# A hybrid decoder layer: one sum moved from VectorE to ScalarE and GpSimd, attention's queued steps re-spaced, and read-backs placed two weight pairs ahead

## The chip, the cores and the metric

The kernel runs on one core of a Trainium2 chip. A core has TensorE (PE, the matrix engine), VectorE (DVE), ScalarE (ACT), GpSimd (POOL) and SyncE (SP, which here issues nearly all transfers). The engines run side by side and wait for one another through semaphores. The metric is the time of one execution on the device in microseconds; lower is better. The median of three runs before the change is 1590.85 us.

## The reference

One layer of a decoder is computed for 1024 prompt tokens and 32 sample tokens (8 sequences of 4), with a model width of 1024, all in float32. In short form:

```
u = rmsnorm(x, norm_pre)
aq, af, ai, aog, az, bq, bk, bv, bz, ga, gb = split(u @ w_in)
fg = lb + (1 - lb) * sigmoid(af)                      # branch A: gated recurrence, 8 heads of 128
S[t] = fg[t] * S[t-1] + (1 - fg[t]) x ai[t];  o[t] = silu(aq[t]) . S[t]
oa = rmsnorm(o) * hgrn_norm * sigmoid(aog) * silu(az)
p = softmax with sink(q . k / 8 + relative bias)       # branch B: window 128, 16 query heads, 2 kv heads
ob = (p . v) * silu(bz)
m = sigmoid(ga) * (oa @ w_pa) + sigmoid(gb) * (ob @ w_pb)
x = x + rmsnorm(m @ w_o, norm_post)
x = x + (p_l @ w_ple) * sigmoid(x @ w_ple_gate)
```

It returns x, the final recurrent states and the last 128 keys and values, for prompt and sample tokens.

## The kernel before

Everything is held transposed: features on the 128 partitions, tokens along the free dimension. To keep float32 accuracy every product is made of three matmuls on rounded parts (high x high, high x low, low x high), so "a matmul" below is one 128 x 128 weight tile times 512 tokens.

**The work by stages.** After the norm and a first head (to about 157 us) the kernel goes through the heads of branch A, one per about 83.5 us. Each head has three weight pairs (F with Q, V with the output gate, the widening gate with the merge gate A). Then come one pair for keys and values, eight attention pairs (bq with bz, about 37.3 us each), four pairs for merge gate B (`gate_b`), and from about 1138 us on the plain products of `gemm` (line 1440): w_pa, w_pb, w_o, w_ple and w_ple_gate.

**One weight pair** is `pair_gemm` (line 377). Of the eight blocks along the contraction six are multiplied by a scheme with seven products P1, P5, P6, P3, P7, P2, P4 (nine matmuls each), two blocks plainly (four stretches of six matmuls): 87 matmuls. Three PSUM banks, `a`, `c` and `b`, serve two output columns (0 and 1) and two token halves ("tiles"). Sums that two outputs share are copied out by ACT as `c1`, `p5` and `u2` (line 409). Right after P6 the second column's plain products for the first token half go into bank `b`, and line 456 adds them to the kept `p5`: one DVE instruction that reads the bank. Then P3 follows in bank `c`, P7 in `a`, and P2 in a new tile in the bank of `b`, so P2 can begin only when line 456 has read it. Line 416 makes the outputs (three per pair), DVE again; that of column 1 adds `p5` to `a`, and P4 goes on in `a` after it. `ctile` (line 228) gives passing tiles from a ring of three.

**What is queued beside the pairs.** Branch A's recurrence (`hgrn_chain`, line 836), the attention (`attention`, line 1134) and the sample tokens' attention (line 1239) are generators in three queues. `pair_gemm` calls `tick()` after every `quantum` matmuls (6 in branch A, 2 in attention and `gate_b`) and once at its end; at a tick the first generator of each queue does its next step if its delay, in ticks, has run out. `yield n` sets that delay, `yield <function>` waits until the function is true. PE executes in the order in which the program emits (line 127); the other engines' order, and that of the transfers, is set by a planner that takes an instruction when it would be ready by its own clock.

**Branch A's end** (lines 1001 to 1022): per head 8 + 7 matmuls give `bO`; ACT squares it and sums; then `bs` is taken from the same ring of two PSUM tiles (`double`, `single`, line 713) for the sample tokens, its matmuls (lines 1014 and 1016) follow at once, and the norm comes after.

**Attention** per pair: line 1341 (ACT) and line 1342 (DVE) build `stk` from the first output; `scores` (queue 1) then makes the logits of two of four token groups (lines 1157 and 1161; DVE line 1165, ACT line 1172, DVE line 1179), and again after the third output. `outs` (queue 0) takes each group 15 ticks after its logits (`A_WAIT[1]`): `turn` 0 transposes into the one PSUM tile `pt` (line 1189) and DVE copies it out, `A_WAIT[2]` ticks later `turn` 1 uses the same PSUM tile and ACT copies it, `A_WAIT[3]` ticks later `values` multiplies (line 1204), then `gated` writes the result (line 1210) and sends it off, and `A_WAIT[4]` ticks pass before the next group. `A_WAIT[0]` lies between two logits.

**After attention** `sample_attention` is queued, three `gate_b` pairs run, `drain()` ticks until the queues are empty, the memory of `sp` is closed, and the eight `oar` tiles (branch A's results, written to DRAM earlier) are read into its place; then comes the fourth `gate_b`.

Of the kernel before, what the change touches and what calls it, by code (L numbers as in the profile page):

```python
# [16 lines left out]
ALU = mybir.AluOpType  # L17
# [13 lines left out]
VAR = ("B11", "T1", "T2", "B21", "T3", "B22", "T4")  # L31
QUANTUM = 6
A_QUANTUM = 2
A_WAIT = (7, 15, 2, 3, 2)
H_WAIT = (2, 4, 6)
AHEAD = 3
WARM = (7, 21, 9)
# [83 lines left out]
def tile_decoder_step(ctx: ExitStack, tc: tile.TileContext, x_prompt, x_sample, state_hgrn, cache_k, cache_v,  # L121
# [4 lines left out]
    V, S, G, T, DM = nc.vector, nc.scalar, nc.gpsimd, nc.tensor, nc.sync  # L126
# [61 lines left out]
    def enqueue(gen, delay=1, q=0):  # L188
        queues[q].append([gen, delay])
# [38 lines left out]
    def ctile():  # L228
        return gt.tile([P, HT], F32, name=tname("ct"), tag="ct", bufs=3)
# [147 lines left out]
    def pair_gemm(W, X, eps, quantum=QUANTUM):  # L377


        n = [0]  # L380

        def mm(ps, a, b, start, stop):
            T.matmul(ps, a, b, start=start, stop=stop, skip_group_check=True)  # L383
            n[0] += 1
            if n[0] % quantum == 0:
                tick()

        def product(ps, key, var, start):
            prepared()
            wh, wl = W.v[key]  # L390
            xh, xl = X.v[var]
            for k in range(M):
                for m, (a, b) in enumerate(((wh, xh), (wh, xl), (wl, xh))):
                    mm(ps, a[:, k, :], b[:, k, :], start and k == 0 and m == 0, k == M - 1 and m == 2)

        def plain(ps, j, t, start):
            if not R:
                return
            wh, wl = W.v["R"]
            xh, xl = X.v["R"]  # L400
            sl = slice(HT * t, HT * t + HT)
            for k in range(R):
                i, q = k // (4 - M), k % (4 - M)
                for m, (a, b) in enumerate(((wh, xh), (wh, xl), (wl, xh))):
                    mm(ps, a[:, i, q, j, :], b[:, k, sl], start and k == 0 and m == 0, k == R - 1 and m == 2)

        def kept(tag, ps):
            t = gt.tile([P, HT], F32, name=tname(tag), tag=tag, bufs=1)
            S.copy(t, ps)
            return t  # L410

        def out(j, t, ps, other):
            lo = HT * t
            into = getattr(eps[j], "into", None)
            dst = into(slice(lo, lo + HT)) if into else ctile()
            V.tensor_tensor(dst, ps, other, op=ALU.add)  # L416
            if into is None:
                eps[j](lo, slice(lo, lo + HT), dst)

        if W.plain:  # L420
            for j in range(2):
                ps = [bank(banks[0]), bank(banks[1])]
                banks.append(banks.pop(0))
                banks.append(banks.pop(0))
                for i in range(2):
                    prepared()
                    wh, wl = W.v[i, j]
                    for t in range(2):
                        xh, xl = X.v[(("T3", "B11"), ("B22", "B21"))[i][t]]
                        for k in range(M):  # L430
                            for m, (a, b) in enumerate(((wh, xh), (wh, xl), (wl, xh))):
                                mm(ps[t], a[:, k, :], b[:, k, :], i + k + m == 0, not R and i == 1 and k == M - 1 and m == 2)
                    if i + j == 0:
                        gs, part = sample_products(W.raw, X.s)
                if j == 0:
                    sample_outputs(gs, part, eps)
                for t in range(2):
                    plain(ps[t], j, t, False)
                    eps[j](HT * t, slice(HT * t, HT * t + HT), ps[t])
            tick()  # L440
            return
        ta, tc_, tb = banks
        a = bank(ta)
        product(a, "P1", "B11", True)
        gs, part = sample_products(W.raw, X.s)
        c1 = kept("c1", a)
        c = bank(tc_)
        product(c, "P5", "T1", True)
        p5 = kept("p5", c)
        product(a, "P6", "T2", False)  # L450
        sample_outputs(gs, part, eps)
        u2 = kept("u2", a)
        if R:
            b = bank(tb)
            plain(b, 1, 0, True)
            V.tensor_tensor(p5, b, p5, op=ALU.add)  # L456
        product(c, "P3", "B22", False)
        plain(c, 0, 0, False)
        out(0, 0, c, u2)
        product(a, "P7", "T3", False)  # L460
        out(1, 0, a, p5)
        b = bank(tb)
        product(b, "P2", "B21", True)
        plain(b, 0, 1, False)
        out(0, 1, b, c1)
        product(a, "P4", "T4", False)
        plain(a, 1, 1, False)
        eps[1](HT, slice(HT, NP), a)
        banks[:] = [tc_, tb, ta]
        tick()  # L470
# [365 lines left out]
    def hgrn_chain(h, F4, QP, K, vn, Gt):  # L836
# [123 lines left out]
        b = to_natural(K, kn, S.copy)  # L960
# [7 lines left out]
        b = double()  # L968
# [11 lines left out]
        b = single()  # L980
# [6 lines left out]
        for g in range(2):  # L987
# [5 lines left out]
            b = single()  # L993
# [12 lines left out]
        for c in range(NC):  # L1006
            o = bO[:, c * P:(c + 1) * P]
            T.matmul(o, att[:, c, :], vn[:, c, :], start=True, stop=c == 0)
            if c > 0:
                T.matmul(o, QE[:, c * P:(c + 1) * P], St[:, c - 1, :], start=False, stop=True)  # L1010
        for c in range(NC):
            S.activation(junk, bO[:, c * P:(c + 1) * P], AF.Square, accum_out=ssh[:, c:c + 1])
        bs = single()
# [12 lines left out]
        b = double()  # L1026
# [3 lines left out]
        b = single()  # L1030
# [103 lines left out]
    def attention(c, stk, zt):  # L1134
# [78 lines left out]
        def scores(gs_):  # L1213
            for g in gs_:
# [4 lines left out]
                scored[n] = now[0]  # L1219
                yield A_WAIT[0]  # L1220

        def outs():
            for g in range(4):
                n = 4 * c + g
                yield lambda: n in scored and now[0] >= scored[n] + A_WAIT[1]
                p0 = turn(g, 0)
                yield A_WAIT[2]
                p1 = turn(g, 1)
# [5 lines left out]
                done.add(("out", n))  # L1234
                yield A_WAIT[4]

# [91 lines left out]
    for c in range(KT):  # L1328
        stk, zt, parts_ = [None, None], [None, zt1[:, c % 2, :]], []

        def ep_bq(ci, sl, ps):
            if ci == NP:
                S.activation(qS[:, :, :, c], ps.rearrange("p (b t) -> p b t", b=8), AF.Copy, scale=0.125)
                return
            t = ci // HT
            settle(("logits", 4 * c - 3 + 2 * t))
            s = stk[t] = sp.tile([P, 2, HT], F32R, name=f"stk{c}_{t}", tag=("vn", "G")[t])
            for j in range(2):
                r = slice(64 * j, 64 * j + 64)
                o = slice(64 - 64 * j, 128 - 64 * j)  # L1340
                S.activation(s[r, j, :], ps[r], AF.Copy, scale=-0.125)
                V.scalar_tensor_tensor(s[o, j, :], ps[r], -0.125, s[r, j, :], op0=ALU.mult, op1=ALU.subtract)  # L1342
            if t == 0:
                parts_[:] = attention(c, stk, zt)
                enqueue(parts_[0](range(2)), 1, q=1)
                enqueue(parts_[1](), 1)
            else:
                enqueue(parts_[0](range(2, 4)), 1, q=1)

        def ep_bz(ci, sl, ps):  # L1350
            if ci == 0:
                settle(("out", 4 * c - 3))
                zt[0] = sp.tile([P, HT], F32, name=f"zt0_{c}", tag="vS")
            if ci == HT:
                settle(("out", 4 * c - 5))
            d = ctile()[:, :32] if ci == NP else zt[ci // HT]
            S.activation(d, ps, AF.Tanh, scale=0.5)
            V.scalar_tensor_tensor(zS[:, c, :] if ci == NP else d, d, 1.0, ps, op0=ALU.add, op1=ALU.mult)
            done.add(("zt", c, ci // HT))

        pair_gemm(b_pairs[c], u, (ep_bq, ep_bz), quantum=A_QUANTUM)


    def gate_b(p):
        def ep_gb(i):
            def ep_(ci, sl, ps):
                sg = ctile()[:, :ps.shape[-1]]
                S.activation(sg, ps, AF.Tanh, scale=0.5)
                V.tensor_scalar(sg, sg, 0.5, 0.5, op0=ALU.mult, op1=ALU.add)
                DM.dma_start(gb_d[i][:, sl], sg)  # L1370
            return ep_

        pair_gemm(gb_pairs[p], u, (ep_gb(2 * p), ep_gb(2 * p + 1)), quantum=A_QUANTUM)

    enqueue(sample_attention(), 1)
    for p in range(3):
        gate_b(p)
    drain()
    aps_es.close()
# [3 lines left out]
    def load_staged(d, n):  # L1383
        out = []
        for i in range(KT):
            out.append(stg.tile([P, NTOK], F32, name=f"{n}{i}", tag=f"s{i}"))
            DM.dma_start(out[i], d[i])
        return out

    oar = load_staged(oa_d, "oar")  # L1390
    gate_b(3)
    for es in (xv_es, gt_es, wp_es, psg_es):
        es.close()
# [282 lines left out]
```

## Time and profile before

| | us |
|---|---|
| median of three runs (lowest, highest) | 1590.85 (1590.65, 1591.33) |
| the profiled execution's own time | 1589.28 |
| its span, first to last instruction | 1587.5 |

| stage | window, us | length | PE busy | DVE busy | ACT busy | POOL busy |
|---|---|---|---|---|---|---|
| a head of branch A | 324.6 to 408.0 | 83.4 | 81.18 | 57.36 | 36.12 | 33.72 |
| another attention pair | 914.3 to 951.6 | 37.3 | 35.27 | 27.08 | 20.20 | 8.15 |
| start of the plain products | 1138.4 to 1167.3 | 28.9 | 16.10 | 22.80 | 19.60 | 0.00 |
| plain products | 1167.3 to 1440.0 | 272.7 | 272.67 | 87.83 | 59.41 | 0.00 |
| the last stage | 1487.0 to 1587.5 | 100.5 | 96.00 | 34.08 | 25.55 | 0.00 |

Matmuls are pipelined: one of 512 columns lasts about 0.39 us in the records, while the next starts 0.227 us after it. So the start times carry the pace, and a row's bracket, [idle before <- releaser], says how long the engine stood still before it and what ended that. The granted clock of TensorE is 0.988 on average over the execution.

### The profile page before, as it was taken

The page shows a single profiled execution, that of the slowest core. Times are in us where ns is not written, and L with a number is a line of the kernel's source. Part 1 is how long each engine was busy: PE and PEld are TensorE (multiplying, and loading weights), DVE is VectorE, ACT ScalarE, POOL GpSimd, SP SyncE. Part 2 cuts the span into 40 slices and gives each one's busy share as a digit, 9 for nine tenths or more (in the row PEclk, how much of TensorE's full clock was granted, in tenths as well). Part 3 has the DMA queues.
Part 4 walks back from the last instruction along what each step waited for, and adds up shares of the span by engine and source line. Part 5 has one row for each costly group of instructions (what it writes and reads, how often), then busy time and mean ns, then how long its engine had stood idle before and what let it go on. Part 6 is the DMA issues. An engine that isn't in the chain of part 4 may idle for free.

```text
span 1587.5 us, 27717 instructions
## 1 busy us (share of the span) xinstructions
PE 1511.3 (95%) x10569; PEld 1260.0 (79%) x10569; DVE 959.8 (60%) x2102; ACT 653.5 (41%) x1639; POOL 425.9 (27%) x381
## 2 busy tenths in 40 slices
PE   8989999999999999999999999999789999998998
PEld 7767777778787777777666666667689999998998
DVE  7777767585858585764777777754452254227532
ACT  6334444444443534344555555543431122333422
POOL 1374444334353434345222222213100000004100
PEclk9999999999999999999999999999899999999999
DMA  5212121313021212213111111135354544103321
GB/s 181 67 30 87 48 82 42 96 41 96 29 82 55 82 55 69 68 50 93 44 47 47 50 48 47 43 91 194 121 199 138 147 123 146 58 24 100 108 81 55
DMA packets 197249, 129.55 MB, mean 82 GB/s; under 512 B 46324, under 2 KB 184749, under 8 KB 197101
## 3 DMA queue, kind: packets, MB, share of 16 engines
q1 hardware_dynamic: 196300, 127.54, 27.0%
q8 instruction: 83, 1.36, 0.4%
q14 instruction: 50, 0.40, 0.1%
q0 software_dynamic: 672, 0.18, 0.1%
q10 hardware_dynamic: 144, 0.07, 0.0%
HBM read 96.89 MB, written 31.88 MB: 81 GB/s over the span
## 4 chain that ended last, share of the span: by engine, by line
PE 67%; DVE 19%; ACT 5%; issue 4%; POOL 3%; DMA 1%; SPq 1%; DVEq 0%; ACTq 0%; POOLq 0%
PE g L383 29%; PE g L1440 23%; ACT lg L1172 2%; PE po L1204 2%; PE gs L365 2%; DVE QE L893 2%; DVE wl L271 1%; DVE ct L416 1%; PE g L790 1%; POOL vS L991 1%; DVE stk L1342 1%; PE pt L1189 1%; PE d L970 1%; DVE S L996 1%; PE lp L1157 1%
## 5 line engine op out<-in xcount | busy, mean ns | idle before, releaser
L271 POOL TENSOR_TENSOR wl<-raw,wh 128x384 fp32r<-128x384 f32 x106 | 118.8, 1124 | 226.0 <-ACT wh L270 207.6
L383 PE MATMUL g<-HT,wh 128*128 128x512 f32 x420 | 173.3, 413 | 0.0
L383 PE MATMUL g<-LT,wh 128*128 128x512 f32 x420 | 168.2, 401 | 0.0
L383 PE MATMUL g<-HT,wl 128*128 128x512 f32 x420 | 166.1, 395 | 0.0
L383 PE MATMUL g<-HB,wh 128*128 128x512 f32 x342 | 140.7, 411 | 9.5 <-DVE p L456 9.5
L383 PE MATMUL g<-LB,wh 128*128 128x512 f32 x342 | 137.5, 402 | 0.0
L383 PE MATMUL g<-HB,wl 128*128 128x512 f32 x342 | 134.6, 393 | 0.0
L271 DVE TENSOR_TENSOR wl<-ws,wh 128x384 fp32r<-128x384 f32 x136 | 94.7, 696 | 51.0 <-ACT wh L270 50.0
L383 PE MATMUL g<-HR,wrh 128*128 128x512 f32 x288 | 118.3, 411 | 0.0
L270 ACT CAST wh<-ws 128x384 fp32r<-128x384 f32 x136 | 69.5, 511 | 111.9 <-PE g L383 74.4
L383 PE MATMUL g<-HR,wrl 128*128 128x512 f32 x288 | 114.7, 398 | 0.0
L383 PE MATMUL g<-LR,wrh 128*128 128x512 f32 x288 | 113.1, 393 | 0.0
L270 ACT CAST wh<-raw 128x384 fp32r<-128x384 f32 x110 | 56.3, 514 | 113.7 <-PE g L383 107.9
L383 PEld LDWEIGHTS g<-HT,wh 128*128 128x128 f32 x420 | 79.5, 189 | 29.2 <-issue 6.6
L1578 POOL TENSOR_TENSOR yT<-yT,acc 128x1056 f32<-128x1056 f32 x4 | 12.9, 3261 | 320.8 <-ACT acc L1574 320.8
L383 PEld LDWEIGHTS g<-HT,wl 128*128 128x128 f32 x420 | 79.6, 190 | 17.3
L383 PEld LDWEIGHTS g<-LT,wh 128*128 128x128 f32 x420 | 79.8, 190 | 15.6 <-issue 1.4
L1418 ACT CAST wh<-raw 128x1024 fp32r<-128x1024 f32 (+1 forms) x40 | 36.8, 920 | 129.7 <-PE g L1440 122.5
L383 PEld LDWEIGHTS g<-HB,wh 128*128 128x128 f32 x342 | 64.5, 189 | 30.1 <-DVE p L456 12.4
L1172 ACT ACTIVATE lg<-lg,mx 128x256 f32<-128x256 f32 (+1 forms) x128 | 62.0, 486 | 51.7 <-DVE mx L1165 51.7
L281 POOL TENSOR_TENSOR ws<-raw 128x384 f32<-128x384 f32 x34 | 37.2, 1093 | 146.2 <-DVE wl L271 92.9
L1419 DVE TENSOR_TENSOR wl<-raw,wh 128x1024 fp32r<-128x1024 f32 (+1 forms) x40 | 46.4, 1163 | 49.5 <-ACT wh L1418 49.5
(393 smaller groups left out, 3988.6 us busy)
## 6 DMA issues: line engine op xcount, KB each, us to landing
raw<-in_w_in_dram SPq DMA_DIRECT2D x116, 256.0 KB
raw<-in_w_in_dram SPq DMA_DIRECT2D x64, 128.0 KB
oa_d<-G SPq DMA_DIRECT2D x8, 528.0 KB
oar<-oa_d SPq DMA_DIRECT2D x8, 528.0 KB
sga<-ga_d SPq DMA_DIRECT2D x8, 528.0 KB
obr<-ob_d SPq DMA_DIRECT2D x8, 528.0 KB
ma_d<-sga SPq DMA_DIRECT2D x8, 528.0 KB
gbr<-gb_d SPq DMA_DIRECT2D x8, 528.0 KB
```

Source lines behind the costliest of these rows:

```text
L270: S.copy(h, x)
L271: eng.tensor_tensor(l, x, h, op=ALU.subtract)
L281: G.tensor_tensor(s, a, b, op=op)
L365: T.matmul(gs[r, :2 * P], xs[:, k, :], raws[k // 4][:, k % 4].rearrange("p j m -> p (j m)"), start=k < 4, stop=k >= 4, tile_position=(0, 3 ...
L383: T.matmul(ps, a, b, start=start, stop=stop, skip_group_check=True)
L416: V.tensor_tensor(dst, ps, other, op=ALU.add)
L893: V.tensor_tensor(Q16[:, :, j, :], src, T44[:, :, 0:1].broadcast_to([P, 64, 4]), op=ALU.mult)
L1172: S.activation(lg[:, j, w, lo:], lg[:, j, w, lo:], AF.Exp, bias=mx[:, 0, 2 * j + w:2 * j + w + 1], scale=-1.0, accum_out=mx[:, 3, 2 * j + ...
L1204: T.matmul(po[r, lo:hi], vN[:, kb, r], pT[:, j, lo:hi], start=i == 0, stop=i == len(items) - 1, skip_group_check=True, tile_position=(0, 6 ...
L1418: S.copy(wh[:, :kt, :], raw3)
L1419: V.tensor_tensor(wl[:, :kt, :], raw3, wh[:, :kt, :], op=ALU.subtract)
L1440: T.matmul(ps, a[:, k, :], b(k)[:, sl], start=k == 0 and m == 0, stop=k == kt - 1 and m == 2)
```

## The change

It makes four edits.

- `pair_gemm`: the sum that line 456 made on DVE is split. ACT copies bank `b` into a passing tile, POOL adds that tile to `p5`.
- `hgrn_chain`: one tick is put between the matmuls of `bO` and what follows them (the squares, then `bs`).
- Attention: `A_WAIT` goes from (7, 15, 2, 3, 2) to (7, 15, 4, 4, 1), and the logits are queued with a delay of 3 ticks in place of 1.
- The third `gate_b` pair is moved behind the reads of `oar`: `drain()`, the closing of `sp` and the eight reads now come after two `gate_b` pairs.

```diff
-A_WAIT = (7, 15, 2, 3, 2)
+A_WAIT = (7, 15, 4, 4, 1)
...
         if R:
             b = bank(tb)
             plain(b, 1, 0, True)
-            V.tensor_tensor(p5, b, p5, op=ALU.add)
+            t = ctile()
+            S.copy(t, b)
+            G.tensor_tensor(p5, p5, t, op=ALU.add)
         product(c, "P3", "B22", False)
...
                 T.matmul(o, QE[:, c * P:(c + 1) * P], St[:, c - 1, :], start=False, stop=True)
+        yield 1
         for c in range(NC):
             S.activation(junk, bO[:, c * P:(c + 1) * P], AF.Square, accum_out=ssh[:, c:c + 1])
...
                 parts_[:] = attention(c, stk, zt)
-                enqueue(parts_[0](range(2)), 1, q=1)
+                enqueue(parts_[0](range(2)), 3, q=1)
                 enqueue(parts_[1](), 1)
             else:
-                enqueue(parts_[0](range(2, 4)), 1, q=1)
+                enqueue(parts_[0](range(2, 4)), 3, q=1)
...
     enqueue(sample_attention(), 1)
-    for p in range(3):
+    for p in range(2):
         gate_b(p)
     drain()
...
     oar = load_staged(oa_d, "oar")
+    gate_b(2)
     gate_b(3)
```

## The prediction, made before the result was known

> **What bounds the kernel now.** I read the page's busy shares first, then a head of branch A and an attention pair among the windows (length, then busy us of PE, its weight loads, DVE, ACT, POOL).
>
> ```profile
> PE 1511.3 (95%) x10569; PEld 1260.0 (79%) x10569; DVE 959.8 (60%) x2102; ACT 653.5 (41%) x1639; POOL 425.9 (27%) x381
> ```
> ```profile
> 241.00:324.60 83.60, 81.18 (x661) 64.12 (x660) 56.44 (x120) 36.02 (x96) 34.20 (x31) 1.00 0.21 65
> 877.00:914.30 37.30, 35.30 (x215) 25.42 (x214) 27.09 (x75) 20.19 (x61) 8.16 (x8) 1.00 0.20 50
> ```
>
> PE works 95% of the span and the change removes no matmul. So only time in which PE stands still can be won, and the next view is who made PE wait (total us, times, longest):
>
> ```profile
> PE g L383 <- DVE p L456: 9.5, 7, 1.4
> PE pt L1189 <- DVE pTs L1193: 8.2, 7, 1.2
> PE g L1440 <- ACT oH L1450: 7.6, 1, 7.6
> PE lp L1157 <- DVE stk L1342: 4.9, 10, 1.3
> PE d L1014 <- DVE S L996: 4.9, 6, 0.9
> PE po L1204 <- ACT pTs L1193: 1.9, 8, 0.2
> PE rsp L1270 <- DMA relw<-in_rel_bias_dram: 1.3, 2, 0.9
> PE d L1014 <- DVE setup L1092: 0.9, 1, 0.9
> ```
>
> The edits touch all of these but the third: 9.5 at line 456, 4.9 + 0.9 = 5.8 at line 1014, 8.2 + 4.9 + 1.9 = 15.0 in attention, and by its timing the 1.3 at the sample attention's table. These 31.6 us are nearly the most that can come back.
>
> **Edit 1: the sum off DVE.** The wait falls once in each of seven heads, in the pair of V and the output gate. PE, DVE and POOL there:
>
> ```profile
> 247.30 0.39 PE L383 MATMUL g<-LR,wrh 128*128 128x512 f32 x1
> 247.53 0.40 PE L383 MATMUL g<-HR,wrl 128*128 128x512 f32 x1
> ...
> 254.87 0.50 PE L383 MATMUL g<-HB,wh 128*128 128x512 f32 x1 [1.35 <-DVE p L456]
> 255.76 0.89 PE L900 MATMUL d<-RB,K 128*32 128x48 f32 x64
> ```
> ```profile
> 252.21 0.71 DVE L879 TENSOR_TENSOR K<-K,Tb 128x528 f32<-128x528 f32 x1
> 253.97 0.28 DVE L887 COPY_PREDICATED attS<-cst,d 32x8 f32<-32x8 int32 x1
> 254.04 0.77 DVE L456 TENSOR_TENSOR p<-g,p 128x512 f32<-128x512 f32 x1
> 255.30 0.70 DVE L416 TENSOR_TENSOR ct<-g,p 128x512 f32<-128x512 f32 x1
> ```
> ```profile
> 249.26 2.35 POOL L271 TENSOR_TENSOR wl<-raw,wh 128x384 fp32r<-128x384 f32 x2
> 256.61 1.02 POOL L281 TENSOR_TENSOR ws<-raw 128x384 f32<-128x384 f32 x1 [5.01 <-DVE wl L271]
> ```
>
> Bank `b` is complete at 247.9 (247.53 + 0.40), but DVE comes to it only at 254.04, behind the recurrence's elementwise work, and P2, which needs the bank, starts 1.35 late. PE's pace is 0.23 us a matmul (247.53 - 247.30). The old and the new operations cost, by the groups of the same shape, and with them one DVE line's range (least, median, most ns) and ACT at the place:
>
> ```profile
> L456 DVE TENSOR_TENSOR p<-g,p 128x512 f32<-128x512 f32 x34 | 24.0, 706 | 7.7 <-PE g L383 7.3
> L409 ACT COPY p<-g 128x512 f32<-128x512 f32 x34 | 19.6, 577 | 0.0
> L820 POOL TENSOR_TENSOR G<-G,ct 128x512 f32<-128x512 f32 x16 | 20.7, 1296 | 18.4 <-DVE ct L819 18.4
> L903 DVE TENSOR_TENSOR K<-K,Tb x8: 684/1454/1465, 78.5 to 674.0; 128x512 f32<-128x512 f32 x8
> 248.76 0.26 ACT L734 COPY vn<-gt 32x128 f32<-32x128 f32 x1 [3.07 <-PE gt L733]
> ```
>
> ACT gets 34 x 0.58 = 20 us, POOL 34 x 1.30 = 44, DVE loses 34 x 0.71 = 24. ACT stands idle for 3.07 ahead of 248.76, so the copy runs from 247.9 to 248.5 and P2 no longer waits for the bank. POOL's two sums run from 249.26 to 251.61; with the new one POOL is done by 252.9. Line 416, which needs `p5`, ran at 255.30, or at 254.6 without line 456 ahead of it: 1.7 us of cover. If that were gone, P4, which goes on in the bank that line 416 reads, would wait.
>
> What is late next is line 900, 0.89 after P2's start (255.76 - 254.87): it would come at 254.87 - 1.35 + 0.89 = 254.41 and needs line 887, done at 254.25. That is 0.16 to spare, in a stretch where DVE never pauses. And POOL slows DVE: line 903 takes 0.68 in the one head where POOL stands still and 1.45 in the others, beside POOL's sum at 256.61, so +0.77. With POOL busy until 252.9, line 879 at 252.21 (0.71, POOL idle now) is the one that I expect to be stretched: line 887 ends 0.77 later, PE waits 0.61 at line 900, and 0.74 of the 1.35 is left. Bounds per head: none (two instructions stretched) and 1.35. I take 0.8, a little above the worked value, because POOL may also let the sum in ahead of its other two: 7 x 0.8 = 5.6 us, bounds 0 and 9.5. The other pairs of a head, attention's and the gates' show no wait for line 456, so there it is worth nothing. The ring of passing tiles gets one user more per pair; the tile three places later is at the earliest the second output's, which needs that sum anyway: nothing.
>
> **Edit 2: one tick before the squares.**
>
> ```profile
> 297.07 0.37 PE L1014 MATMUL d<-vn,attS 32*32 32x128 f32 x2 [0.67 <-DVE S L996]
> ...
> 297.93 0.50 PE L383 MATMUL g<-HB,wh 128*128 128x512 f32 x1
> 298.27 0.40 PE L383 MATMUL g<-LB,wh 128*128 128x512 f32 x1
> ```
> ```profile
> 295.82 1.11 DVE L996 SCALAR_TENSOR_TENSOR S<-S,Tb,d 128x128 f32<-128x128 f32 x4
> ```
>
> `bs` needs the PSUM tile that line 996 reads until 296.93. A tick puts six matmuls, 6 x 0.23 = 1.4 us, ahead of line 1014, which waits for 0.67, so the wait is covered. It also adds one more change between kinds of matmuls: the first step after one is 0.34 us (298.27 - 297.93) against 0.23, and it has two sides, so I put it at 0.25: 8 heads x 0.25 = 2.0. Sum: 5.8 - 2.0 = 3.8 us, bounds 2.0 and 5.8. The squares can now run while PE goes on, so the norm behind them is no later against its six ticks.
>
> **Edit 3: attention's steps.** PE, then DVE:
>
> ```profile
> 879.61 0.60 PE L1189 MATMUL pt<-cst,lg 128*128 128x128 f32 x4
> 882.27 0.44 PE L1189 MATMUL pt<-cst,lg 128*128 128x128 f32 x2 [1.14 <-DVE pTs L1193]
> 906.59 0.61 PE L1157 MATMUL lp<-KK,stk 128*128 128x128 f32 x3 [0.39 <-DVE stk L1342]
> ```
> ```profile
> 880.74 0.69 DVE L1342 SCALAR_TENSOR_TENSOR stk<-ct,stk 64x512 fp32r<-64x512 f32 x1
> 881.55 0.66 DVE L1193 COPY pTs<-pt 128x512 f32<-128x512 f32 x1
> ```
>
> The second transposes need the first's PSUM tile; DVE copies it only at 881.55, behind `stk`. Four ticks in place of two give 4 matmuls, 0.91 us, more: of each wait (8.2 / 7 = 1.17) 0.91 goes, 7 x 0.91 = 6.4. The logits' delay gives the same 0.91: of the row's 4.9 all goes but what the longest wait (1.3) has over it: 4.5. One tick more for ACT's copy, 0.45, covers its 1.9 / 8 = 0.24: 1.9. Together 12.8, if everything else kept its place. It doesn't. By the queue's rules a group took 2 + 3 + 2 ticks and two for its conditions, 9; now 4 + 4 + 1 and two, 11. Four groups take 44 ticks, just what a pair has (87 matmuls at 2 a tick, and the closing one). So `outs`, until now paced by the 15 ticks after the logits, falls back two matmuls per pair and meets other DVE bursts in every pair. By this count no `settle` comes to run ticks without matmuls (the closest, for `zt0`, is met 7 matmuls early in the last pair). I leave 3.5 us, something over a quarter, to new waits: 9.3 us, bounds 0 and 15.0.
>
> **Edit 4: the reads of `oar`.** The SP queue, and ACT's first use:
>
> ```profile
> 1104.52 1.04 SPq L1387 DMA_DIRECT2D oar<-oa_d  x2
> ```
> ```profile
> 1144.80 7.89 ACT L1450 CAST oH<-oar 128x1056 fp32r<-128x1056 f32 x8
> ```
>
> The last reads are issued at 1104.5 already, inside the third gate pair, though the code has them behind it, and used at 1144.8, when the last gate pair has freed the memory that `oH` goes to. So reading earlier brings nothing, and the 7.6 us stay. What the move could harm: the third pair's six stores and the fourth pair's weights may now stand behind eight reads on SP, 4 x 1.04 = 4.2 us of issue, against a pair of 87 x 0.23 = 20 us. And `drain()` has two pairs to hide in. By the count attention's last `values` come 35 matmuls later and the sample attention's last matmuls 34, at 76 of the second gate pair's 87: it ends 11 matmuls before the drain, and its eight stores (at the reads' 0.52 each, 4 us) run under the third pair. I take 0, bounds -2 and +1. The table's loads can start 28 matmuls later, the matmuls that wait for them come 34 later: six matmuls, 1.4 us, of slack against a wait of 1.3; I take half, 0.7.
>
> **The sum.** 5.6 + 3.8 + 9.3 + 0 + 0.7 = 19.4 us. The profiled execution took 1589.28, its span 1587.5, and 1.8 lie around it: 1569.9 for a like execution. The median of the runs is 1.57 above that execution, so I forecast 1590.85 - 19.4 = 1571.4. About 0.2%, 3.2 us, can be told from no change.
>
> **The rivals.** *A, the waits come back elsewhere in attention.* With `outs` exactly as slow as the pair and drifting, each turn meets the `stk` burst in some pair. For: DVE is busy 27 of 37 us there. Against: of 32 second transposes only 7 waited at two ticks' distance. Attention and the table then give 0: 5.6 + 3.8 = 9.4 won, 1581.4 us.
>
> *B, slower: POOL's sums hold DVE wherever they run.* If in each of 34 pairs a DVE instruction stands still for all of a 1.30 us sum and PE waits for it, 44.2 us are lost against 19.4 won: 1615.6. The sign turns at 19.4 / 34 = 0.57 us per pair. For: line 903's +0.77. Against: PE's waits for DVE are few, so most of DVE's work has slack, and DVE loses the 0.71 of line 456 in every pair. The Trainium skill, "SBUF — State Buffer", section "Who interferes with whom", says that a DVE instruction with two SBUF inputs and a POOL instruction that reads SBUF contend, and that the loser blocks rather than shares. That speaks for this rival; the trace agrees as far as line 903 goes, 0.68 against 1.45.
>
> *C, no change*: the heads' gain goes to line 900, attention's comes back, and the move costs its 2: 0 + 3.8 - 2 = 1.8 won, 1589.0.
>
> **How the numbers follow.** Forecast 0.68, A 0.16, C 0.08, B 0.08. Faster: 0.68 + 0.16 = 0.84; same 0.08; slower 0.08. All bounds at their best give 31.6 won; that together is unlikely, so I stop 2.7 short: 1562. The upper end takes A in, with 0.43 per head at line 456 in place of 0.8, 2.6 us worse: 1584.
>
> **What would show it.** Right: no wait for `p` in PE's list, line 900 waiting some 0.6 us per head, none at line 1014, a head near 82.3 in place of 83.6, an attention pair near 36.1 in place of 37.3; POOL's busy time up by some 44 us, DVE's down by less than 24. Wrong: waits at lines 1189 or 1157 as long as now at other places (A); P4 waiting for POOL's sum, or DVE's mask and `wl` instructions longer in all pairs with PE behind them (B); PE idle between the second and third gate pair (the drain uncovered).

## The result, and the profile after the change

The changed kernel takes 1570.86 us (median of 4 runs, 1569.41 to 1572.04) beside 1590.75 for the kernel before in 4 runs: a ratio of 0.9878, 95% interval 0.9861 to 0.9896. The forecast was 1571.4. The profiled execution took 1569.41, its span 1567.6, which is 19.9 less than before. Lines behind 456 have moved down by two, behind 1010 by three and behind 1390 by four; below, line numbers are those of the kernel under discussion.

The windows of a head and of an attention pair after the change (length, then busy us of PE, its weight loads, DVE, ACT, POOL):

```profile
238.50:320.60 82.10, 80.90 (x662) 64.30 (x661) 56.68 (x117) 37.58 (x99) 38.67 (x34) 1.00 0.22 66
863.10:899.80 36.70, 35.02 (x218) 26.01 (x216) 26.85 (x78) 20.68 (x63) 8.48 (x8) 1.00 0.20 51
```

And who made PE wait (total us, times, longest):

```profile
PE d L902 <- DVE attS L889: 8.8, 8, 1.2
PE g L1444 <- ACT oH L1454: 7.8, 1, 7.8
PE pt L1192 <- DVE pTs L1196: 6.4, 3, 3.3
...
PE g L383 <- DVE ct L416: 2.4, 1, 2.4
PE po L1207 <- ACT pTs L1196: 2.2, 2, 1.5
PE g L383 <- ACT c L409: 1.4, 1, 1.4
```

Read beside the list of before, it shows what went and what came. The waits for `p` (9.5) and for `S` (5.8) are gone. In their place stand line 902 (the old line 900), where PE now waits for DVE's masks in every head, three long waits at attention's second transposes in place of seven short ones, and a stop of 2.4 in a gate pair, which the kernel before didn't have.

Where the time came from is read from marks that both kernels have: the first matmul of line 365 in each pair. Before, then after (the marks end the heads, attention with two gate pairs, and the third gate pair; the last row is the first plain product):

```profile
743.29 1.07 PE L365 MATMUL gs<-raw,xs 128*32 128x256 f32 x16
1097.37 1.07 PE L365 MATMUL gs<-raw,xs 128*32 128x256 f32 x16
1118.85 1.07 PE L365 MATMUL gs<-raw,xs 128*32 128x256 f32 x16
1145.92 0.66 PE L1440 MATMUL g<-oH,wh 128*128 128x352 f32 x1 [7.56 <-ACT oH L1450]
```
```profile
733.10 1.07 PE L365 MATMUL gs<-raw,xs 128*32 128x256 f32 x16
1075.53 1.07 PE L365 MATMUL gs<-raw,xs 128*32 128x256 f32 x16
1099.68 1.07 PE L365 MATMUL gs<-raw,xs 128*32 128x256 f32 x16
1127.02 0.66 PE L1444 MATMUL g<-oH,wh 128*128 128x352 f32 x1 [7.83 <-ACT oH L1454]
```

The heads give 743.29 - 733.10 = 10.2. The stretch from the first to the second row (attention and the first two gate pairs; "the attention stretch" below) was 354.08 long and is 342.43: 11.65. The third gate pair was 21.48 and is 24.15: 2.7 lost. The way to the plain products loses 0.3 and what follows gains 1.0. Together 19.9.

### The profile page after: what moved, and what is told of

It is laid out like the page before. It is cut to its first block, busy times and chain, and to the rows that moved or that the text cites. A ratio compares the mean times of both kernels' runs of the same rounds, so it can differ in the third digit from the quotient of the medians.

```text
span 1567.6 us, 27727 instructions
## 1 busy us (share of the span) xinstructions
PE 1504.2 (96%) x10569; PEld 1261.3 (80%) x10569; DVE 942.0 (60%) x2068; ACT 667.9 (43%) x1673; POOL 468.5 (30%) x415
## 4 chain that ended last, share of the span: by engine, by line
PE 74%; DVE 17%; issue 3%; ACT 3%; DMA 2%; POOL 1%; SPq 0%; DVEq 0%; ACTq 0%; POOLq 0%
PE g L383 32%; PE g L1444 25%; PE gs L365 2%; PE po L1207 2%; DVE QE L895 2%; PE g L792 2%; DVE ct L416 1%; PE pt L1192 1%; PE d L1010 1%; PE d L972 1%; PE lp L1160 1%; DVE stk L1345 1%; PE d L1012 1%; DVE QE L854 1%; PE lp L1164 1%
## 5 line engine op out<-in xcount | busy, mean ns | idle before, releaser
L383 PEld LDWEIGHTS g<-HT,wl 128*128 128x128 f32 x420 | 79.2, 189 | 17.8 <-issue 0.9
```

## The experiments

Each was timed beside the kernel before. Where times can't tell two kernels apart, their marks are compared.

**One edit at a time.** Four kernels, each the kernel before with one edit of the four as the change's diff has it. The sum alone:

> The sum on ACT and POOL alone, the rest as before. Theory: in the V pair of each of seven heads the wait for line 456's bank (1.35 us) goes, and nearly all of it comes back at the matmuls of line 902, because POOL's extra sum stretches two DVE instructions (the K products, lines 878 and 879 before) by about 1 us in all. The V pair then shortens by 0.3 to 0.4 us per head: 2 to 3 us in all, 1588 us. Rival 1, the prediction's value: 0.8 per head, 5.6 us, 1585. Rival 2: the sum is worth nothing by itself because it costs attention its DVE time: 1590.8 or above.

Measured: 1588.77, ratio 0.9992 (0.9978 to 1.0007). By the marks the pair of V and the output gate falls from 28.44 to 28.09 in each of seven heads, 2.4 in all; from there on no other pair changes by more than 0.1, but for one of 32.65 that takes 32.21. PE's list has

```profile
PE d L902 <- DVE attS L889: 8.7, 8, 1.2
```

so 1.17 to 1.21 of the 1.35 that the old wait took stands at line 902 now. The time alone can't be told from no change. The tick alone:

> One tick between the matmuls of bO and what follows, the rest as before. Theory: the whole stop at line 1014, about 1.06 us from one start to the next beyond the pace, goes in every head and one change between kinds of matmuls costs about 0.2: 0.85 us per head, 7 to 8 us in all, 1583 us. Rival, the prediction's value: 3.8 us, 1587, since the waits view shows 5.8 and each change costs 0.25.

Measured: 1582.65, ratio 0.9957 (0.9942 to 0.9972). The pair with the tick falls from 32.17 to 31.31, and the waits for `p` stay. That is the theory's value, not the 3.8 of the prediction. Attention's spacing and delay alone:

> A_WAIT (7, 15, 4, 4, 1) and the logits' delay of 3, the rest as before (three gate pairs ahead of the drain). Theory: attention's eight pairs gain 9 to 10 us and the wait for the relw loads (1.35) goes: 10 to 11.5 us, 1580 us, with long waits at line 1189 in only two to four pairs, where the drifting turn meets the logits' reductions and the stk instructions on DVE. Rival: half of that is owed to the sum being off DVE, since DVE sets attention's pace: 5 us, 1586.

Measured: 1575.61, ratio 0.9913 (0.9898 to 0.9927). The attention pairs have the lengths of the changed kernel (35.34, 35.65, 36.72, 34.55, 35.03, 37.09, 35.57 against 37.33), the third gate pair is 21.48 as before. The gain is the theory's and not the rival's half: attention does as well with line 456 on DVE. The reads' place alone:

> Two gate pairs, then the drain and the eight reads, then two gate pairs, the rest as before. Theory: the reads share the transfer engines with the stores of the third pair's gates, whose passing tiles are held longer, so PE stops for 1 to 2.5 us inside the third gate pair; the start of the plain products may give about 1 back: 0 to 2 us slower, 1591 to 1593. Rival, the prediction's value: nothing, 1590.8, with no stop in the third gate pair.

Measured: 1590.67, ratio 1.0008 (0.9993 to 1.0024), third gate pair 21.48. The stop that was expected there didn't come. So the stop of 2.4 comes from none of the edits alone.

**The sum by DVE, late.** ACT's copy stays, POOL's sum goes, DVE adds from SBUF where the sum is first needed:

```diff
             t = ctile()
             S.copy(t, b)
-            G.tensor_tensor(p5, p5, t, op=ALU.add)
...
+        if R:
+            V.tensor_tensor(p5, p5, t, op=ALU.add)
         out(1, 0, a, p5)
```

> The changed kernel, but DVE does the sum, from ACT's copy in SBUF and late, just ahead of the output that needs it; POOL gets nothing new. Theory (POOL's sum, running beside DVE's two K instructions, stretched these by 1.0 us, and PE pays it at line 902): these two come back to about 1.2 and 0.7 us, the seven waits of 1.2 at line 902 fall to 0.2 or less, and about 1.0 us per head more is won, 7 in all: 1564. Rival (the recurrence's chain is late there whoever adds, because PE merely arrives 1.35 sooner): line 902 still waits 0.8 or more, and the time stays at 1570 to 1571. Second rival: the 0.7 us of DVE in each of 34 pairs, given back, costs PE elsewhere, in attention above all: 1572 or more, with new waits for line 416 or the logits' tiles.

Measured: 1566.06, ratio 0.9841 (0.9825 to 0.9857). Then the same with the third gate pair back in its place ahead of the drain, which is also tried by itself:

```diff
-    for p in range(2):
+    for p in range(3):
         gate_b(p)
...
     oar = load_staged(oa_d, "oar")
-    gate_b(2)
     gate_b(3)
```

> The changed kernel without edit 4: three gate pairs stand before the drain again, the reads of oar behind them. Theory (the eight reads in one run on SP, ahead of the third gate pair's first stores, hold the ring of passing tiles): the stop of 2.4 us at line 383 in the third gate pair goes, the wait for oH gets shorter by about the same or stays, and the time falls by 2 us, to 1569. Rival (the stop comes from edit 1's fourth user of the ring of three tiles, wherever the reads are): the stop stays, 1571.

Measured: 1570.36, ratio 0.9867 (0.9853 to 0.9882).

> The changed kernel with DVE's late sum and without edit 4, both at once. If both theories hold and do not overlap: 1571 less 7 less 2, 1562, with neither the waits at line 902 nor the stop in the third gate pair. If only the first holds 1564, if only the second 1569.

Measured: 1564.72, ratio 0.9832 (0.9811 to 0.9854). For DVE's late sum the theory holds, in the mechanism and in six of seven heads. First the two instructions in question and POOL beside them in the changed kernel, with the end of the masks and PE's stop:

```profile
247.95 1.47 POOL L458 TENSOR_TENSOR p<-p,ct 128x512 f32<-128x512 f32 x1
248.53 1.47 DVE L880 TENSOR_TENSOR K<-K,F 128x528 f32<-128x528 f32 x1
249.39 1.48 POOL L271 TENSOR_TENSOR wl<-raw,wh 128x384 fp32r<-128x384 f32 x1
250.03 1.40 DVE L881 TENSOR_TENSOR K<-K,Tb 128x528 f32<-128x528 f32 x1
...
252.47 0.28 DVE L889 COPY_PREDICATED attS<-cst,d 32x8 f32<-32x8 int32 x1
...
252.91 0.89 PE L902 MATMUL d<-RB,K 128*32 128x48 f32 x64 [1.20 <-DVE attS L889]
```

Then the same two in the kernel with both edits, and its waits in the whole span:

```profile
247.81 1.19 DVE L881 TENSOR_TENSOR K<-K,F 128x528 f32<-128x528 f32 x1
...
249.03 0.71 DVE L882 TENSOR_TENSOR K<-K,Tb 128x528 f32<-128x528 f32 x1
```
```profile
PE gt L740 <- DVE ct L416: 1.9, 7, 0.3
PE d L903 <- DVE attS L890: 1.8, 5, 1.0
```

Without POOL's sum the two are back at 1.19 and 0.71, 0.97 shorter, and line 903 waits 1.8 in place of 8.8. The size falls short of the 7 us expected: the pair of V goes from 28.09 to 27.40 in six heads, 0.7 per head and 4.2 in all, because `ct` of line 416 comes behind DVE's sum and PE waits 0.26 for it at line 740. In the first of the seven the two instructions are back as well, but DVE comes to them 0.8 later in the pair than in the other heads: line 903 waits 0.96 there, and the pair stays at 28.17.

For the place of the third gate pair the theory holds in the trace: with it back, the pair is 21.48 in both kernels and the plain products start 3.4 sooner than in the changed kernel (1123.62 against 1127.02). In the times, 1570.36 stands beside 1570.86 and the intervals of the ratios overlap. In the profiled execution 3.0 went again in the plain products and the last stage, which the edit doesn't touch; 1.5 of it comes with a stretch of 3.4 us at half clock (the last section tells of these) that the changed kernel's profile doesn't have there. So the gain is shown in the trace and open in the time.

**Without edit 1.** DVE adds from PSUM as before; the other three edits stay.

```diff
-            t = ctile()
-            S.copy(t, b)
-            G.tensor_tensor(p5, p5, t, op=ALU.add)
+            V.tensor_tensor(p5, b, p5, op=ALU.add)
```

> The changed kernel without edit 1: DVE adds from PSUM at once as before, edits 2, 3 and 4 stay. If edit 4 stops the third gate pair by itself once attention's spacing has moved the sample attention later: the stop of 2.4 us stays, and with edit 1's 2.3 gone the time is 1573. If the stop needs edit 1's additional user of the ring of passing tiles: no stop, and 1571, so that edit 1 with edit 4 is worth nothing in all. The waits of 1.35 at line 456 come back in the seven heads in both cases.

Measured: 1575.14, ratio 0.9895 (0.9878 to 0.9912). PE's list:

```profile
PE g L383 <- DVE ct L416: 3.4, 1, 3.4
```

The stop stays, so it doesn't need edit 1's user of the ring. The kernels that have it are those with edits 3 and 4; edit 3 without 4 and edit 4 without 3 don't. (Those that have it also have edit 2; no kernel has 3 and 4 without it.) The changed kernel at the place, SP's queue, ACT, DVE and PE:

```profile
1077.33 5.25 SPq L1390 DMA_DIRECT2D oar<-oa_d  x8
1083.40 34.59 SPq L1373 DMA_DIRECT2D gb_d<-ct  x11
```
```profile
1093.10 0.63 ACT L1371 ACTIVATE ct<-ct 128x512 f32<-128x512 f32 x1 [2.41 <-DMA gb_d<-ct]
1093.27 0.69 DVE L416 TENSOR_TENSOR ct<-g,p 128x512 f32<-128x512 f32 x1 [2.00 <-DMA gb_d<-ct]
1094.02 0.50 PE L383 MATMUL g<-HT,wh 128*128 128x512 f32 x1 [2.37 <-DVE ct L416]
```

The eight reads go out in one run, ahead of the pair's stores. A passing tile is free only when its store has landed; DVE waits for such a tile, and PE for the bank that DVE is to read. The eight reads bring 528 KB each, and from 1083 to 1090 the transfers run at 372 to 435 GB/s. No store was issued between 1084.70 and 1094.32, so the one that DVE waits for took more than 8 us to land. With the third pair ahead of the drain the reads go out as 2, 4 and 2 between the stores. With edit 4 and the old spacing they went as 2, 1 and 5, and as late as 1091 to 1100.

**Attention's two halves.** Four kernels on the version with both edits above (DVE's late sum, third pair ahead of the drain; A_WAIT (7, 15, 4, 4, 1), delay 3). No drift:

```diff
-A_WAIT = (7, 15, 4, 4, 1)
+A_WAIT = (7, 15, 4, 3, 1)
```

> DVE's late sum, three gate pairs before the drain, and A_WAIT (7, 15, 4, 3, 1): a group's steps take ten ticks in place of eleven, four groups 40 of a pair's 44, so that they are paced again by the 15 ticks after the logits. To be compared with the kernel that differs only in the fourth number (4). Theory (the waits of 3.4, 1.8 and 1.3 us for the first turn's copy are the price of the drift): all attention pairs come to the same length, these three waits go, and 5 us are won, 1559.7 beside 1564.7; the gate pair that shrank to 30.8 as the drifted steps ran out of it may go back by 1 or 2. Rival (what meets DVE's bursts is a matter of place, not of drift): a wait stands at one place of every pair, 0.5 us or more, seven times, and the time is the same or 1 to 4 us longer.

Measured: 1558.93, ratio 0.9808 (0.9786 to 0.9830), 5.8 less than with the drift, or 3.8 by the ratios to the kernel before, where the theory had 5 (by the intervals of the ratios the two aren't told apart, by the marks they are: attention is 4.3 shorter). The waits of 1.8 and 1.3 went, the wait of 3.4 in the first pair stayed, and a wait of 0.3 came in each of the other pairs. The spacing with the old delay:

```diff
-                enqueue(parts_[0](range(2)), 3, q=1)
+                enqueue(parts_[0](range(2)), 1, q=1)
...
-                enqueue(parts_[0](range(2, 4)), 3, q=1)
+                enqueue(parts_[0](range(2, 4)), 1, q=1)
```

> DVE's late sum, three gate pairs before the drain, A_WAIT as in the changed kernel, but the logits' delay of 1 in place of 3. To be compared with the kernel with delay 3. Theory of the prediction (0.91 us more ahead of each wait for stk, 4.5 in all): the waits at the logits for stk, 3.3 us in all, go up to about 5 to 7, longest 1.1 or more, and the time by 2 to 4 us, to 1568. Rival (the bursts on DVE that the logits wait behind are longer than the delay, or the delay only moves the steps against the pair's end): the waits stay within 1 us of 3.3 and the time at 1564 to 1566.

Measured: 1579.52, ratio 0.9944 (0.9926 to 0.9962), 14.8 more than with the delay of 3, or 17.8 by the ratios: the theory's direction at four times its size. The waits for `stk` are 14.3 where 5 to 7 were expected. The delay with the old spacing:

```diff
-A_WAIT = (7, 15, 4, 4, 1)
+A_WAIT = (7, 15, 2, 3, 2)
```

> DVE's late sum, three gate pairs before the drain, the logits' delay of 3 kept, but A_WAIT as before the change, (7, 15, 2, 3, 2): edit 3's delay without its spacing. Beside it stand the kernels with both halves (1564.7, attention 11.8 us shorter than before) and with the spacing alone (1579.5, attention 4.6 us longer than before). The prediction's view (two halves that add, 4.5 from the delay and 6.4 + 1.9 less 3.5 from the spacing): the waits for stk are nearly gone, the waits of 1.2 for the second turn stay as in the kernel before, and attention is 4 to 5 us shorter than before: 1572. Rival (the halves are one step: with the steps of outs where they were, a later logits step meets another burst): new waits of 0.5 us or more at the logits or the values in every pair, and attention as long as before or longer: 1576 or more.

Measured: 1588.42, ratio 0.9994 (0.9984 to 1.0004). The rival's time holds, with 12 more than it asked for, and the view that the halves add is refuted. The place that the rival named does not hold: the new waits stand at the second turn, not at the logits or the values. Ten ticks divided otherwise:

```diff
-A_WAIT = (7, 15, 4, 4, 1)
+A_WAIT = (7, 15, 5, 2, 1)
```

> As the kernel with A_WAIT (7, 15, 4, 3, 1), but (7, 15, 5, 2, 1): still ten ticks a group and no drift, the second turn one tick later, the values one tick sooner after it. The seven waits of 0.3 us that stand at the second turn there should go, 0.45 us of cover being added: 2 us less, 1557. Against it: the values then have one tick less for ACT's copy, which was 0.24 us late at three ticks in the kernel before; if that comes back in each of 32 groups, 1 to 7 us are lost, 1560 to 1566.

Measured: 1553.30 (1552.32 to 1554.61), ratio 0.9773 (0.9759 to 0.9786), the shortest of all, 17.6 less than the changed kernel, or 16.7 by the ratios; the seven waits went and ACT's didn't come. Of the 6.9 by which attention is shorter than with (7, 15, 4, 3, 1), 4.7 lie in the seven pairs and 3.2 in the first, where the wait falls from 3.4 to 1.8 and no half clock follows; the two gate pairs take 0.9 longer. The attention stretch in these kernels, by the same marks, with the stretches of 3.4 us at half clock that begin inside it:

| A_WAIT | delay | attention stretch, us | at half clock |
|---|---|---|---|
| (7, 15, 2, 3, 2), the kernel before | 1 | 354.08 | 1 |
| (7, 15, 2, 3, 2) | 3 | 367.73 | 5 |
| (7, 15, 4, 4, 1) | 1 | 358.74 | 6 |
| (7, 15, 4, 4, 1) | 3 | 342.25 | 1 |
| (7, 15, 4, 3, 1) | 3 | 337.93 | 2 |
| (7, 15, 5, 2, 1) | 3 | 331.02 | 1 |

Each half alone makes attention longer than before, by 13.7 and 4.7; both together make it 11.8 shorter. A part of that is the clock: without its five additional stretches at half clock, about 8 us, the spacing alone would be some 3 shorter than before; the delay alone would still be some 7 longer. No kernel has neither half together with the late sum, so the kernel before, with line 456 on DVE, stands for it; with both halves the way of the sum moves the stretch by 0.6 at most (341.82 on DVE as before, 342.43 on POOL, 342.25 late). PE's waits in the stretch, for the last five rows in the table's order:

```profile
PE pt L1193 <- DVE pTs L1197: 26.9, 16, 4.2
PE lp L1161 <- DVE stk L1346: 3.5, 9, 0.4
```
```profile
PE lp L1161 <- DVE stk L1346: 14.3, 22, 1.4
PE pt L1193 <- DVE pTs L1197: 2.5, 3, 1.1
```
```profile
PE pt L1193 <- DVE pTs L1197: 6.4, 3, 3.4
PE lp L1161 <- DVE stk L1346: 3.3, 8, 0.6
PE po L1208 <- ACT pTs L1197: 2.2, 2, 1.5
```
```profile
PE pt L1193 <- DVE pTs L1197: 5.6, 8, 3.4
PE lp L1161 <- DVE stk L1346: 0.7, 2, 0.4
```
```profile
PE pt L1193 <- DVE pTs L1197: 1.8, 1, 1.8
PE lp L1161 <- DVE stk L1346: 0.8, 2, 0.4
```

What a delay without spacing meets is seen on DVE and PE in that kernel:

```profile
873.67 0.69 DVE L1346 SCALAR_TENSOR_TENSOR stk<-ct,stk 64x512 fp32r<-64x512 f32 x1
...
875.23 1.23 DVE L1183 TENSOR_TENSOR lg<-lg,mx 128x1024 f32<-128x1024 f32 x1
876.48 0.69 DVE L1346 SCALAR_TENSOR_TENSOR stk<-ct,stk 64x512 fp32r<-64x512 f32 x1
877.20 0.76 DVE L320 TENSOR_TENSOR wrl<-raw,wrh 128x256 fp32r<-128x256 f32 x2
877.88 0.68 DVE L1197 COPY pTs<-pt 128x512 f32<-128x512 f32 x1
```
```profile
874.67 0.60 PE L1193 MATMUL pt<-cst,lg 128*128 128x128 f32 x4
878.71 0.41 PE L1193 MATMUL pt<-cst,lg 128*128 128x128 f32 x2 [2.75 <-DVE pTs L1197]
```

The first turn's transposes are done at 875.3, but DVE has the scaling of a softmax (line 1183), `stk` and a weight split queued ahead of the copy. Once in every pair the second turn waits 2.7 for that (4.2 in the first). In the changed kernel's drift the same copy is late in three pairs only: by 3.3 behind a scaling of 2.0, by 1.8 and 1.3 behind two `stk`. Without the drift the pairs are alike, 34.91 to 34.97 in six of seven, with a wait of 0.3 each, and the tick that the last kernel moves takes that too: 34.35 to 34.40 in all seven.

## Why the prediction was right, point by point

The time and the sum were right, 19.4 forecast and 19.9 found; the terms were not. That the sum came so close is luck: edit 1 fell 3.2 short and edit 4 lost 2.7, edit 2 gave 4.2 too much and edit 3 with the table 1.65.

**Edit 1: 5.6 forecast, 2.4 found.** The step that failed is that line 879 "is the one that I expect to be stretched: line 887 ends 0.77 later, PE waits 0.61 at line 900". POOL let the sum in between its other two, at 247.95, which the forecast had as a chance for better, and that made it worse: the sum and the second `wl` behind it lie beside both K instructions, which grow by 0.28 and 0.69. PE waits 1.20. Per head 0.35 is left of 1.35, near the bound that stood there as "two instructions stretched" and not at the 0.8 that was taken. That POOL is the cause is shown by the kernel with DVE's late sum, in six heads of seven. The Trainium skill, "SBUF — State Buffer", section "Who interferes with whom", names this pair of instructions as contending; the trace agrees that they do, but not that the loser stands still for the whole of the other: beside 2.95 us of POOL the two DVE instructions grew by 0.97. Rival B had that as its price, and no other pair lost anything.

**Edit 2: 3.8 forecast, 8.0 found** by the marks (7.4 in the kernel with the tick alone). Two steps failed. The 2.0 taken off for the change between kinds of matmuls isn't there: the pair lost 0.86, more than the whole wait of 0.67. And the waits list understates a stop, since a matmul's record lasts 0.39 while the next is due after 0.227: at line 456 it shows 1.35, but the matmul ahead of it had started at 253.12, so the start is 254.87 - 253.12 - 0.23 = 1.52 late. The rest is in head 0, where the same tick takes a stop of 1.76 apart:

```profile
133.25 1.45 PE L1028 MATMUL d<-cst,on 128*128 128x128 f32 x8 [1.76 <-ACT on L1021]
```
```profile
133.80:137.20 3.40, 3.40 (x12) 2.52 (x11) 3.09 (x4) 1.47 (x4) 2.01 (x2) 0.51 0.02 7
```

Behind that stop the kernel before ran 3.4 us at half clock (0.51 in the window's clock column; matmuls of 512 columns start 0.43 apart, at 135.46, 135.89 and 136.31). In the changed kernel the wait is 0.31, a wait of 1.44 follows, and the clock stays whole: 1.45 is won there.

**Edit 3: 9.3 and 0.7 for the table forecast, 11.65 found.** Right within its bounds, and wrong in its working. "The logits' delay gives the same 0.91: of the row's 4.9 all goes but what the longest wait (1.3) has over it: 4.5" failed. Added up from start to start over seven pairs, all steps to and among the first logits matmuls took 21.72 before and 21.54 after: 0.2 came, and 2.3 in the first pair (5.23 and 2.93). The transposes gave 7.9 + 1.5 = 9.4 (6.4 forecast), with 3.0 of new waits from the drift already in it, ACT's copy 0.7 (1.9 forecast). The two halves were taken to add, and the last experiments show that they don't. The drift was foreseen, and its 3.5 was of the right size, 3.0 in the seven pairs, and 3.3 at the first pair, where the longest stop before was 1.3. But the forecast saw it as a fixed price, while it can be had back: 4.3 in the kernel without drift, 11.2 in the last.

**Edit 4: 0 forecast, -2.7 found.** The bounds were -2 and +1, so it fell outside. The step that failed is "4 x 1.04 = 4.2 us of issue, against a pair of 87 x 0.23 = 20 us": the reads were counted by their issue on SP, not by what the stores behind them need to land. The ring's additional user, which the forecast put at nothing, isn't the cause, since the stop stays without edit 1. The reads stood in one run because edit 3 had moved the sample attention, and so the memory that they go to, later against the pairs (the first read comes 1.8 behind the third gate pair's mark, and 5.7 ahead of it with edit 4 alone): an interaction that the parts, costed one by one, couldn't show.

**The rivals.** A (the waits come back elsewhere) is half true: new waits, no loss of the gain. C's two mechanisms both happened, for edit 1 in most of its size and for edit 4 in full; what it missed is that attention's gain stayed. B didn't happen. Of the signs, a head is 82.1 (82.3 forecast), the seven attention pairs are 35.8 on average (36.1), POOL gained 42.6 (44) and DVE lost 17.8 (less than 24: 0.97 per head went into the two K instructions, 6.8 in seven heads).

## What to carry to other kernels

Steps that share a queue with another engine's bursts don't add up: a distance and a delay that each cost time alone can win together, so cost them as one placement, and try the neighbouring placements (one tick moved from one distance to the next made attention 7 us shorter here). An instruction moved to an idle engine isn't free for the engine that it leaves: POOL's sum stretched the DVE instructions beside it by 0.97 us a head. Look at what runs beside it in the stage where the wait ends. Cost a run of reads by what the transfers behind it need to land, and who waits for that.

## What the runs showed of the hardware

**The granted clock changes on a grid, and it follows how full the last window of the grid was.** In each of the 14 traces all changes of the clock lie on one grid with steps of 3.41 us. The kernel with the delay alone shows what that does. Its second turn has the same stop of 2.7 in seven pairs, but the stops fall differently on the grid. Windows of the grid around two of them (PE busy comes second, the clock is the third number from the end):

```profile
795.39:798.81 3.42, 2.15 (x12) 1.47 (x10) 2.98 (x7) 3.19 (x10) 0.00 (x0) 1.00 0.01 2
798.81:802.22 3.41, 1.95 (x12) 1.67 (x14) 2.38 (x5) 0.38 (x1) 0.00 (x0) 1.00 0.00 0
802.22:805.63 3.41, 3.41 (x32) 1.77 (x31) 2.42 (x12) 2.31 (x10) 0.00 (x0) 1.00 0.02 5
```
```profile
836.35:839.76 3.41, 1.01 (x6) 0.91 (x7) 3.25 (x7) 1.14 (x3) 0.00 (x0) 1.00 0.01 2
839.76:843.17 3.41, 3.41 (x14) 2.21 (x14) 1.30 (x7) 0.77 (x3) 0.00 (x0) 0.50 0.00 0
```

The first stop is split over two windows, with 1.27 and 1.46 idle, and the clock stays whole. The second empties one window by 2.40, and the next 3.4 us run at 0.50. It goes so by turns in all seven pairs.

Narrow matmuls leave a window empty too. Take the columns of the matmuls that start in a window, as a share of what the pace of 0.227 us for 512 columns would put there. Of all windows at full clock in the 14 traces, half clock follows in 75 of 78 with a share under 0.30, in 29 of 111 from 0.30 to 0.45, and in none of 5968 above. So the seven stops of 1.35 in the kernel before do nothing (shares of 0.51 and more), while in the last kernel half clock follows at 1049.57 on a window without any stop, which matmuls of 32 columns fill (share 0.30). The share describes these traces; what the chip itself counts isn't shown, and between 0.30 and 0.45 the share doesn't decide.

What half clock costs is read from the pace. In the kernel with the spacing and the old delay:

```profile
894.14 0.63 PE L383 MATMUL g<-HT,wh 128*128 128x512 f32 x1
894.57 0.63 PE L383 MATMUL g<-LT,wh 128*128 128x512 f32 x1
```

The step is 0.43 us in place of 0.23. That costs 3.4 x (1 - 0.227 / 0.43) = 1.6 us per window. Of the 16.5 us by which the delay of 1 lengthens attention, the waits list explains 5.5, and five more such stretches about 8. The Trainium skill, "TensorE: Matmul & The Clock Gate", section "What's actually happening", has the clock fall to half after an idle window of about 3.4 us. The trace agrees with the two levels and with the 3.4, but a window needn't be wholly idle: 2.40 of 3.41 was enough above.
